# A residual block on eight cores: narrower weight chunks, saves of bf16 weights partly deferred and recorded later, constants on another queue, two x buffers in place of three

## Chip, cores, metric

The kernel runs on all 8 cores of one Trainium2 chip. Each core computes four of the 32 sequences, 16 tiles of 512 tokens, and exchanges no data with the others. The metric is the device time of the slowest core, in microseconds (us). Some runs fall in a second, slower state, in which one die's cores show a lower granted clock: one run of the kernel before took 4140 us with four cores at 0.834 to 0.839 and the other four at 0.983 to 0.987.

In the views, PE is TensorE (the matmuls), PEld its weight loads, DVE VectorE, ACT ScalarE, POOL GpSimd and SP SyncE. `wsrc` is the f32 source of the weights, `wbf` their bf16 copy in HBM, `ring` the slots on chip. The head is the time from the start to the merge stage of the second tile.

## The reference, cut to what matters

```python
xn  = rms_norm(h, norm_mix_pre)
proj = xn @ w_in                       # q, k, v, gMLP u and v, two gates: 1024 -> 3840
attn = banded_sink_attention(q, k, v)  # window 128, 8 query and 2 key heads
gm   = u * (W_s LN(v) + b)             # 128-token chunks
mix  = (sigmoid(g_a) * (attn @ w_a) + sigmoid(g_b) * (gm @ w_g)) @ w_out
h    = h + rms_norm(mix)
hn   = rms_norm(h)
ff   = (silu(hn @ w_gate) * (hn @ w_up)) @ w_down     # 1024 -> 2816 -> 1024
out  = h + rms_norm(ff)
# x is (32, 2048, 1024) float32, weights are float32, depth 1
```

## The kernel before

The weights are not kept on chip: every tile streams them through a ring of four slots, in 31 chunks. They arrive as f32 and are multiplied as bf16. In the first tile each chunk is loaded by a DMA that casts, issued from POOL, and then saved as bf16 in HBM by a DMA from SP. Later tiles reload the bf16 copy. The order of chunks in a tile is: merge M0 to M7, output projection O0 and O1, the next tile's Q, KV, U and VG, gate/up G0 to G10, and the six down chunks D0 to D5 twice (two halves of the tokens).

```python
NCH = 31
CHE = 4096
NSLOT = 4
NTMP = 10
N_CORES = 8
CAST_DMA = True
NXB = 3
# ...
    def record_load(self):
        n = self.n_loaded
        if n >= len(self.order):
            return
        self.n_loaded += 1
        c = self.order[n]
        s = n % NSLOT
        slot = self.ring[s]
        rkeys = [("ring", s, q4) for q4 in range(4)]
        if c not in self.cast_done:
            self.cast_done.add(c)
            if CAST_DMA:
                self.dma(AP(slot, CHE, 0, 128, 0, [(1, CHE)]), AP(self.wsrc_d, CHE, c * 128, 128, 0, [(1, CHE)]),
                         [], rkeys, ("WC", s), q="pool", max_last=8192)
            for q4 in (range(4) if not CAST_DMA else ()):
                si = self.stg_i
                self.stg_i = 1 - si
                stg = AP(self.stg[si], 1024, 0, 128, 0, [(1, 1024)])
                src = AP(self.wsrc_d, CHE, c * 128, 128, 1024 * q4, [(1, 1024)])
                self.dma(stg, src, [], [("stg", si)], ("ST", si))
                dst = AP(slot, CHE, 0, 128, 1024 * q4, [(1, 1024)])
                eng = ("dve", "act", "pool", "dve")[q4]
                if eng == "act":
                    fn = lambda e, o=dst, i=stg: e.activation(out=o, in_=i, func=AF.Copy)
                else:
                    fn = lambda e, o=dst, i=stg: e.tensor_copy(out=o, in_=i)
                self.op(eng, fn, [("stg", si)], [("ring", s, q4)])
            self.dma(AP(self.wbf_d, CHE, c * 128, 128, 0, [(1, CHE)]), AP(slot, CHE, 0, 128, 0, [(1, CHE)]),
                     rkeys, [("wbf", c)], ("WS", s))
        else:
            self.dma(AP(slot, CHE, 0, 128, 0, [(1, CHE)]), AP(self.wbf_d, CHE, c * 128, 128, 0, [(1, CHE)]),
                     [("wbf", c)], rkeys, ("W", s))
# (the branch for not CAST_DMA never runs)
    def chunk_done(self):
        while self.n_loaded < min(self.n_used + NSLOT, len(self.order)):
            self.record_load()
    def load_x(self, t):
        xb = self.xb[t % NXB]
        src = bass.AP(self.x_d, t * TT * D, [[D, 128], [128 * D, NB], [1, D]])
        dst = AP(xb, 4096, 0, 128, 0, [(D, NB), (1, D)])
        self.dma(dst, src, [], [("xb", t % NXB, b) for b in range(NB)], ("X", t % NXB))
    def store_y(self, t):
        xi = t % NXB
        xb = self.xb[xi]
        dst = bass.AP(self.y_d, t * TT * D, [[D, 128], [128 * D, NB], [1, D]])
        src = AP(xb, 4096, 0, 128, 0, [(D, NB), (1, D)])
        self.dma(dst, src, [("xb", xi, b) for b in range(NB)], [("y", t)], ("Y", xi))
# ...
    def record(self):
        n = self.n_tiles
        self.stream_init()
        self.load_x(0)
        self.load_consts(0)
        for _ in range(NSLOT - 1):
            self.record_load()
        self.rms_scale_all(0, 0)
        self.transposes(self.xnT, "xnT", self.g1, "g1")
        self.load_consts(1)
        self.stage_front(0)
        for t in range(1, min(n, NXB)):
            self.load_x(t)
        wo_groups = [[(C_O0, 8)], [(C_O0 + 1, 8)]]
        dn_groups = [[(C_D0, 8), (C_D0 + 1, 8), (C_D0 + 2, 6)], [(C_D0 + 3, 8), (C_D0 + 4, 8), (C_D0 + 5, 6)]]
        for _ in self.stage_attn(0):
            pass
        self.stage_spatial(0)
        for t in range(n):
            xi = t % NXB
            nxt = t + 1 < n
            self.stage_merge(t, inter=self.rms_scale((t + 1) % NXB, 0) if nxt else None)
            if t >= 1 and t - 1 + NXB < n:
                self.load_x(t - 1 + NXB)
            if nxt:
                self.transposes(self.xnT, "xnT", self.g1, "g1")
            self.tokmajor_out(xi, self.mergedT, "mg", wo_groups, self.g2bc, "g2bc", 16,
                              after_pair=lambda pair, xi=xi: self.rms_scale_all(xi, 1, (2 * pair, 2 * pair + 1)))
            hT = lambda: self.transposes(self.hnT, "hnT", self.g3, "g3")
            if nxt:
                self.stage_front(t + 1, mid=hT)
                self.stage_ffn_gu(t, mid=lambda t=t: self.stage_spatial(t + 1))
            else:
                hT()
                self.stage_ffn_gu(t)
            inter = self.stage_attn(t + 1) if nxt else None
            self.tokmajor_out(xi, self.hT, "h", dn_groups, self.g4bc, "g4bc", 16, inter=inter)
            self.store_y(t)
```

A wait is derived for each recorded operation from what it reads and writes, and each engine takes its operations strictly in recorded order. So a chunk's cast, on POOL, waits for the matmuls that read the slot's old chunk and for the save of that old chunk. A save, on SP, waits for its cast, and everything recorded later on SP waits behind it.

The softmax here doesn't subtract the row's maximum and nothing guards it: scores larger than these inputs give would overflow.

Of the kernel before, what the change touches and what calls it, by code (L numbers as in the profile page):

```python
# [23 lines left out]
CAST_DMA = True  # L24
NXB = 3
# [133 lines left out]

def build_wsrc(w_in, w_a, w_g, w_out, w_gate, w_up, w_down):  # L160
# [27 lines left out]
    return np.stack(chunks, axis=0)  # L188

def build_consts(norm_mix_pre, norm_mix_post, norm_ffn_pre, norm_ffn_post, attn_sinks,  # L190
# [6 lines left out]
    for g in range(2):  # L197
        for half in range(2):
            for hh2 in range(2):
# [20 lines left out]
    return {k: np.ascontiguousarray(v, dtype=np.float32) for k, v in c.items()}  # L220

CONST_SHAPES = {"ident": 128, "tbl": 2048, "g1": 8, "g3": 8, "g2bc": 1024, "g4bc": 1024,
                "lngpp": 4, "lnbpp": 4, "bsbc": 512, "sinkbc": 8, "wsT": 512, "cmask": 512}

class Builder:
# [7 lines left out]
    def alloc(self, es):  # L233
# [3 lines left out]
        self.wsrc_d = nc.dram_tensor("wsrc", [NCH * 128, CHE], F32, kind="ExternalInput")  # L237
# [23 lines left out]
        self.stg = [sb("stg%d" % i, 1024, F32) for i in range(2)] if not CAST_DMA else []  # L261
        self.stg_i = 0
# [6 lines left out]
        self.esink = sb("esink", 8, F32)  # L269
        self.wsT = sb("wsT", 512, BF16)  # L270
        self.ident = sb("ident", 128, BF16)
        self.ones = sb("ones", 128, BF16)
        self.g1 = sb("g1", 8, F32)
        self.g3 = sb("g3", 8, F32)
        self.lngpp = sb("lngpp", 4, F32)
        self.lnbpp = sb("lnbpp", 4, F32)
# [57 lines left out]

    def load_consts(self, part):
        ckey = ("C%d" % part,)
        def cdram(name, off=0, n=None):
            F = CONST_SHAPES[name]
            return AP(self.c_d[name], F, 0, 128, off, [(1, n or F)])

        def direct(name, t):
            n = CONST_SHAPES[name]
            self.dma(AP(t, n, 0, 128, 0, [(1, n)]), cdram(name), [], [("c", name)], ckey, bulk=True)

        def via_tmp(name, off, n):
            ti = self.ntmp()
            self.dma(self.T(ti, n), cdram(name, off, n), [], [("tmp", ti)], ckey, bulk=True)
            return ti

        if part == 0:  # L350
            for name, t in (("g1", self.g1), ("g3", self.g3), ("lngpp", self.lngpp), ("lnbpp", self.lnbpp)):
                direct(name, t)
        else:
            for name, t in (("g2bc", self.g2bc), ("g4bc", self.g4bc)):
                direct(name, t)
        if part == 0:
# [3 lines left out]
            ti = via_tmp("ident", 0, 128)  # L360
            self.op("dve", lambda e, o=AP(self.ident, 128, 0, 128, 0, [(1, 128)]), s=self.T(ti, 128):
                    e.tensor_copy(out=o, in_=s), [("tmp", ti)], [("c", "ident")])
        else:
            for q4 in range(4):
                ti = via_tmp("tbl", 512 * q4, 512)
                self.op("dve", lambda e, o=AP(self.tbl, 2048, 0, 128, 512 * q4, [(1, 512)]), s=self.T(ti):
                        e.tensor_copy(out=o, in_=s), [("tmp", ti)], [("c", "tbl")])
            ti = via_tmp("sinkbc", 0, 8)
            self.op("act", lambda e, o=AP(self.esink, 8, 0, 128, 0, [(1, 8)]), s=self.T(ti, 8):
                    e.activation(out=o, in_=s, func=AF.Exp), [("tmp", ti)], [("c", "esink")])  # L370
            self.op("dve", lambda e, o=AP(self.vtok, 650, 0, 128, 0, [(1, 650)]): e.memset(o, 1.0), [],
                    [("v", i) for i in range(5)])
            t3 = via_tmp("wsT", 0, 512)
            t4 = via_tmp("cmask", 0, 512)
            self.op("dve", lambda e, o=AP(self.wsT, 512, 0, 128, 0, [(1, 512)]), a=self.T(t3), b=self.T(t4):
                    e.tensor_tensor(out=o, in0=a, in1=b, op=ALU.mult), [("tmp", t3), ("tmp", t4)], [("c", "wsT")])
            t5 = via_tmp("bsbc", 0, 512)
# [3 lines left out]
            for g in range(4):  # L381
                self.op("dve", lambda e, o=AP(self.B2, 512, 0, 128, 128 * g, [(1, 128)]), i=self.P(bk, 128, 128 * g),
                        s=AP(self.lnbpp, 4, 0, 128, g, [(1, 1)]), b=self.T(t5, 128, off=128 * g):
                        e.scalar_tensor_tensor(out=o, in0=i, scalar=s, in1=b, op0=ALU.mult, op1=ALU.add),
                        [("ps", bk), ("c", "lnbpp"), ("tmp", t5)], [("c", "B2")])

    def stream_init(self):
# [10 lines left out]
        self.cast_done = set()  # L398
        self.n_loaded = 0
        self.n_used = 0  # L400

    def record_load(self):
        n = self.n_loaded
        if n >= len(self.order):
            return
        self.n_loaded += 1
        c = self.order[n]
        s = n % NSLOT
        slot = self.ring[s]
        rkeys = [("ring", s, q4) for q4 in range(4)]  # L410
        if c not in self.cast_done:
            self.cast_done.add(c)
            if CAST_DMA:
                self.dma(AP(slot, CHE, 0, 128, 0, [(1, CHE)]), AP(self.wsrc_d, CHE, c * 128, 128, 0, [(1, CHE)]),
                         [], rkeys, ("WC", s), q="pool", max_last=8192)
            for q4 in (range(4) if not CAST_DMA else ()):
                si = self.stg_i
                self.stg_i = 1 - si
                stg = AP(self.stg[si], 1024, 0, 128, 0, [(1, 1024)])
                src = AP(self.wsrc_d, CHE, c * 128, 128, 1024 * q4, [(1, 1024)])  # L420
                self.dma(stg, src, [], [("stg", si)], ("ST", si))
                dst = AP(slot, CHE, 0, 128, 1024 * q4, [(1, 1024)])
                eng = ("dve", "act", "pool", "dve")[q4]
                if eng == "act":
                    fn = lambda e, o=dst, i=stg: e.activation(out=o, in_=i, func=AF.Copy)
                else:
                    fn = lambda e, o=dst, i=stg: e.tensor_copy(out=o, in_=i)
                self.op(eng, fn, [("stg", si)], [("ring", s, q4)])
            self.dma(AP(self.wbf_d, CHE, c * 128, 128, 0, [(1, CHE)]), AP(slot, CHE, 0, 128, 0, [(1, CHE)]),
                     rkeys, [("wbf", c)], ("WS", s))  # L430
        else:
            self.dma(AP(slot, CHE, 0, 128, 0, [(1, CHE)]), AP(self.wbf_d, CHE, c * 128, 128, 0, [(1, CHE)]),
                     [("wbf", c)], rkeys, ("W", s))

    def next_chunk(self, expect):
# [3 lines left out]
        while self.n_loaded <= n:  # L439
            self.record_load()  # L440
        s = n % NSLOT
        return self.ring[s], [("ring", s, q4) for q4 in range(4)]

    def chunk_done(self):
        while self.n_loaded < min(self.n_used + NSLOT, len(self.order)):
            self.record_load()

    def load_x(self, t):
        xb = self.xb[t % NXB]
        src = bass.AP(self.x_d, t * TT * D, [[D, 128], [128 * D, NB], [1, D]])  # L450
        dst = AP(xb, 4096, 0, 128, 0, [(D, NB), (1, D)])
        self.dma(dst, src, [], [("xb", t % NXB, b) for b in range(NB)], ("X", t % NXB))

# [35 lines left out]
    def transposes(self, dst_t, dkey, gain, gname):  # L489
        for kc in range(8):  # L490
            bk = self.nbank()
            for b in range(NB):
# [7 lines left out]
            gsc = AP(gain, 8, 0, 128, kc, [(1, 1)])  # L500
            self.op("dve", lambda e, o=dst, i=src, s=gsc: e.tensor_scalar(out=o, in0=i, scalar1=s, scalar2=None,
                                                                          op0=ALU.mult),
                    [("ps", bk), ("c", gname)], [(dkey, kc)])
# [172 lines left out]
    def stage_spatial(self, t):  # L676
        for b in range(NB):
# [6 lines left out]
            for gq in range(4):  # L684
                self.op("dve", lambda e, o=self.T(tq, 128, off=128 * gq), i=self.P(bk, 128, 128 * gq),
                        s=AP(self.lngpp, 4, 0, 128, gq, [(1, 1)]), c=AP(self.B2, 512, 0, 128, 128 * gq, [(1, 128)]):
                        e.scalar_tensor_tensor(out=o, in0=i, scalar=s, in1=c, op0=ALU.mult, op1=ALU.add),
                        [("ps", bk), ("c", "lngpp"), ("c", "B2")], [("tmp", tq)])
# [6 lines left out]
    def stage_merge(self, t, inter=None, per_chunk=2):  # L695
        for c in range(8):
# [19 lines left out]
            if inter is not None and c >= 1:  # L716
                for _ in range(per_chunk):
                    next(inter, None)
# [102 lines left out]
    def store_y(self, t):  # L821
        xi = t % NXB
        xb = self.xb[xi]
        dst = bass.AP(self.y_d, t * TT * D, [[D, 128], [128 * D, NB], [1, D]])
        src = AP(xb, 4096, 0, 128, 0, [(D, NB), (1, D)])
        self.dma(dst, src, [("xb", xi, b) for b in range(NB)], [("y", t)], ("Y", xi))

    def record(self):
# [4 lines left out]
        for _ in range(NSLOT - 1):  # L833
            self.record_load()
        self.rms_scale_all(0, 0)
        self.transposes(self.xnT, "xnT", self.g1, "g1")
        self.load_consts(1)
        self.stage_front(0)
        for t in range(1, min(n, NXB)):
            self.load_x(t)  # L840
# [5 lines left out]
        for t in range(n):  # L846
            xi = t % NXB
            nxt = t + 1 < n
            self.stage_merge(t, inter=self.rms_scale((t + 1) % NXB, 0) if nxt else None)
            if t >= 1 and t - 1 + NXB < n:  # L850
                self.load_x(t - 1 + NXB)
            if nxt:
                self.transposes(self.xnT, "xnT", self.g1, "g1")
            self.tokmajor_out(xi, self.mergedT, "mg", wo_groups, self.g2bc, "g2bc", 16,
                              after_pair=lambda pair, xi=xi: self.rms_scale_all(xi, 1, (2 * pair, 2 * pair + 1)))
            hT = lambda: self.transposes(self.hnT, "hnT", self.g3, "g3")
# [7 lines left out]
            self.tokmajor_out(xi, self.hT, "h", dn_groups, self.g4bc, "g4bc", 16, inter=inter)  # L864
            self.store_y(t)
        self.op("sp", None, [("y", t) for t in range(n)], [])
# [70 lines left out]
```

## Time and profile before

| | |
|---|---|
| median of 6 runs, two of them slow | 3589.04 us (the four fast runs 3586.7 to 3590.2) |
| spans of the cores in the profiled run | 3573.9 to 3585.1 us, clock 0.984 to 0.988 |
| PE busy | 3388.8 us, 95% |
| queue of the casts (q0) | 6.3% of the 16 DMA engines' span |
| queue of SP (q1) | 59.3% |

The page of the kernel before divides the span into 40 slices of 90 us; a digit is a busy share in tenths.

```profile
span 3585.1 us, 53875 instructions; the slowest of 8 cores (3573.9 to 3585.1 us)
...
PE   3786899999999999999999999999999999999988
...
DMA  8989956758476574856657475665747557464645
```

PE is short of full in the first five slices and the last two; the DMA row is at 8 or 9 in the same first five. What PE waits for in the first 420 us is listed in the view of waits (engine and tile, what was waited for, us in total, times, longest):

```profile
PE ps L326 <- DMA ring<-wsrc: 56.9, 19, 5.3
PE ps L496 <- DVE xn L480: 34.0, 2, 33.7
PE ps L326 <- DVE wsT L376: 22.2, 1, 22.2
PE ps L326 <- DMA ring<-wbf: 6.1, 1, 6.1
```

The first row are casts that come late, one by one, the third is the constant `wsT`, which stands in PE's order before the first projection, and the last is the first reload of the second down pass.

### The profile page before, as it was taken

Reading aid. Unit: us, or ns where it says so; the run is one execution under the profiler, and the core shown is the slowest. Engines: PE = TensorE matmul, PEld = TensorE weight load, DVE = VectorE, ACT = ScalarE, POOL = GpSimd, SP = SyncE. Lnnn points to the kernel's source line nnn. Section 1 sums busy time; section 2 is a strip of 40 time slices with the busy share of each in tenths; the row PEclk is TensorE's granted clock in tenths of the full one; section 3 lists DMA queues with packets and bytes.
Section 4 is the critical chain, followed back from the end, with each engine's and each line's share of the span. In section 5 each row is a group of like instructions: output and inputs, shape, how many; then the busy total and the mean of one; then the engine's idle time right before and its main releaser. Section 6 shows DMA issues by size and latency. Waiting matters only on the chain.

```text
span 3585.1 us, 53875 instructions; the slowest of 8 cores (3573.9 to 3585.1 us)
## 1 busy us (share of the span) xinstructions
PE 3388.8 (95%) x18129; PEld 1587.2 (44%) x18129; DVE 1338.7 (37%) x2845; ACT 1046.9 (29%) x2130; POOL 408.7 (11%) x427
## 2 busy tenths in 40 slices
PE   3786899999999999999999999999999999999988
PEld 1342344444444444444444444444444444444433
DVE  1341352424435243443424335342443524244332
ACT  1321322323233232323323232332323223232321
POOL 1210110201001020100202011020201102010010
PEclk9899999999999999999999999999999999999999
DMA  8989956758476574856657475665747557464645
GB/s 186 217 190 212 268 180 198 231 168 251 160 232 195 188 244 155 251 167 222 207 183 246 148 250 174 211 221 172 254 153 246 177 200 230 169 225 162 229 144 193
DMA packets 113002, 726.82 MB, mean 203 GB/s; under 512 B 11360, under 2 KB 11488, under 8 KB 36960
## 3 DMA queue, kind: packets, MB, share of 16 engines
q1 hardware_dynamic: 104304, 690.87, 59.3%
q0 software_dynamic: 8432, 32.51, 6.3%
q8 instruction: 154, 2.52, 0.3%
q14 instruction: 112, 0.92, 0.1%
HBM read 689.78 MB, written 66.06 MB: 211 GB/s over the span
## 4 chain that ended last, share of the span: by engine, by line
PE 85%; DMA 8%; DVE 3%; issue 2%; ACT 1%; POOL 1%; SPq 0%; DVEq 0%; ACTq 0%; POOLq 0%
PE ps L326 83%; DMA ring<-wsrc 5%; DMA wbf<-ring 2%; PE ps L496 1%; DVE xb L793 1%; DVE tmp L773 1%; DMA tmp<-c_bsbc 1%; ACT atok L620 1%; PE ps L633 0%; ACT PT L661 0%; POOL stats L785 0%; DVE atok L624 0%; DMA ring<-wbf 0%; SPq L330 0%; DVE attnT L637 0%
## 5 line engine op out<-in xcount | busy, mean ns | idle before, releaser
L326 PE MATMUL ps<-hnT,ring 128*128 128x512 bf16 x5632 | 1224.6, 380 | 23.7 <-DMA ring<-wsrc 23.7
L326 PEld LDWEIGHTS ps<-hnT,ring 128*128 128x128 bf16 x5632 | 550.5, 98 | 688.5 <-issue 31.4
L326 PE MATMUL ps<-xnT,ring 128*128 128x512 bf16 x3328 | 750.8, 381 | 7.2 <-DMA ring<-wsrc 7.2
L326 PE MATMUL ps<-ring,hT 128*128 128x512 bf16 x2816 | 645.0, 383 | 30.4 <-DMA ring<-wsrc 20.6
L817 DVE TENSOR_TENSOR hT<-ps,tmp 128x512 bf16<-128x512 f32 x352 | 240.7, 691 | 798.9 <-PE ps L326 794.9
L326 PEld LDWEIGHTS ps<-xnT,ring 128*128 128x128 bf16 x3328 | 326.4, 98 | 401.7 <-issue 17.9
L813 ACT ACTIVATE tmp<-ps 128x512 f32<-128x512 f32 x352 | 210.2, 597 | 980.7 <-PE ps L326 974.0
L326 PEld LDWEIGHTS ps<-ring,hT 128*128 128x128 bf16 x2816 | 268.4, 99 | 340.6 <-issue 49.2
L785 POOL TENSOR_TENSOR stats<-stats,neghalf 128x2 f32<-128x2 f32 x64 | 44.9, 701 | 2080.9 <-DVE stats L782 2080.9
L326 PE MATMUL ps<-ring,mergedT 128*128 128x512 bf16 x1024 | 226.0, 381 | 7.8 <-DMA ring<-wsrc 5.3
L767 ACT ACTIVATE tmp<-ps 128x512 f32<-128x512 f32 x256 | 150.0, 595 | 262.8 <-PE ps L326 196.3
L710 DVE TENSOR_TENSOR tmp<-ps,tmp 128x512 f32<-128x512 f32 x128 | 88.4, 691 | 339.9 <-PE ps L326 333.2
L793 DVE SCALAR_TENSOR_TENSOR xb<-tmp,stats,xb 128x512 f32<-128x512 f32 x256 | 186.7, 750 | 75.1 <-POOL stats L785 61.1
L715 POOL TENSOR_TENSOR mergedT<-tmp 128x512 bf16<-128x512 f32 x128 | 166.5, 1300 | 413.8 <-DVE tmp L712 307.6
L661 ACT ACTIVATE PT<-ps 128x512 bf16<-128x512 f32 (+1 forms) x256 | 135.3, 581 | 203.9 <-PE ps L326 203.6
L464 ACT ACTIVATE xn<-xb 128x1024 bf16<-128x1024 f32 x128 | 134.3, 1051 | 154.5 <-DVE xb L793 154.4
L705 ACT ACTIVATE tmp<-ps 128x512 f32<-128x512 f32 x128 | 76.4, 597 | 278.9 <-PE ps L326 278.7
L326 PEld LDWEIGHTS ps<-ring,mergedT 128*128 128x128 bf16 x1024 | 100.0, 98 | 127.2 <-issue 11.6
L326 PE MATMUL ps<-ring,xnT 128*128 128x512 bf16 (+1 forms) x1024 | 144.3, 299 | 0.0
L326 PE MATMUL ps<-gmT,ring 128*128 128x512 bf16 x512 | 132.3, 381 | 4.1 <-DVE gmT L692 4.1
L326 PE MATMUL ps<-attnT,ring 128*128 128x512 bf16 x512 | 131.4, 379 | 0.0
L624 DVE TENSOR_SCALAR atok<-ps,stats 128x64 bf16<-128x64 f32 x256 | 72.7, 284 | 147.3 <-ACT atok L620 147.3
(68 smaller groups left out, 2048.3 us busy)
## 6 DMA issues: line engine op xcount, KB each, us to landing
ring<-wbf SPq DMA_DIRECT2D x561, 1024.0 KB, 6.1
xb<-x SPq DMA_DIRECT2D x16, 2048.0 KB, 12.8
y<-xb SPq DMA_DIRECT2D x16, 2048.0 KB, 10.6
ring<-wsrc POOLq DMA_DIRECT2D x31, 1024.0 KB, 24.5
wbf<-ring SPq DMA_DIRECT2D x31, 1024.0 KB, 12.4
tmp<-c_tbl SPq DMA_DIRECT2D x4, 256.0 KB, 21.8
g2bc<-c_g2bc SPq DMA_DIRECT2D x1, 512.0 KB, 12.8
g4bc<-c_g4bc SPq DMA_DIRECT2D x1, 512.0 KB, 19.1
```

What stands on the lines that cost most here:

```text
L326: self.op("pe", lambda e: e.matmul(out, lhsT, rhs, start=start, stop=stop), reads, writes)
L464: self.op("act", lambda e, o=junk, i=src, a=acc: e.activation(out=o, in_=i, func=AF.Square, accum_out=a), [("xb", xi, b)], [("xn", b), ("s ...
L624: e.tensor_scalar(out=o, in0=i, scalar1=s_, scalar2=None, op0=ALU.mult),
L661: e.activation(out=o, in_=s, func=AF.Exp, scale=0.125),
L705: self.op("act", lambda e, o=self.T(ta), s=self.P(bga): e.activation(out=o, in_=s, func=AF.Sigmoid), [("ps", bga)], [("tmp", ta)])
L710: e.tensor_tensor(out=o, in0=a, in1=c, op=ALU.mult), [("ps", bra), ("tmp", ta)], [("tmp", t1)])
L715: e.tensor_tensor(out=o, in0=a, in1=c_, op=ALU.add), [("tmp", t1), ("tmp", t2)], [("mg", c)])
L767: e.activation(out=o, in_=i, func=AF.Square, accum_out=a),
L785: self.op("pool", lambda e, o=ms, h=nh: e.tensor_tensor(out=o, in0=o, in1=h, op=ALU.pow), [mkey, ("c", "neghalf")], [mkey])
L793: e.scalar_tensor_tensor(out=o, in0=i, scalar=s, in1=x_, op0=ALU.mult, op1=ALU.add),
L813: self.op("act", lambda e, o=self.T(tg), s=self.P(bg): e.activation(out=o, in_=s, func=AF.Silu), [("ps", bg)], [("tmp", tg)])
L817: e.tensor_tensor(out=o, in0=a, in1=c, op=ALU.mult),
```

## The change

Its intent is to shorten the start. It (1) stores the source without padding and moves only the used columns of a chunk, (2) casts odd gate/up chunks again in the second tile and saves them only then, (3) records a save three chunks later, (4) issues constants from ACT, packs the small ones, consumes them in the middle of the first projections, and issues chunks 1 to 3 behind the first normalisation, (5) keeps two x buffers, so the next x is loaded in the merge stage behind the old tile's store, and splits loads and stores of a tile by 128-token block. The core of the diff, with cuts:

```diff
-CAST_DMA = True
-NXB = 3
+NXB = 2
# ...
+def SAVE_AT(c):
+    return 0 if c >= C_D0 or c < C_G0 or c % 2 == 0 else 1
+
+CW = ([4096, 3072, 4096, 4096] + [3072] * 8 + [4096] * 2 + [4096] * 11 + [4096, 4096, 3072] * 2)
+OFF = [128 * sum(CW[:c]) for c in range(NCH)]
+NW = 128 * sum(CW)
# ...
-    return np.stack(chunks, axis=0)
+    return np.concatenate([np.ascontiguousarray(ch[:, :CW[c]]).reshape(-1) for c, ch in enumerate(chunks)]).reshape(-1, PW)
# ... (constants: q="act"; tables loaded in part 1, consumed in part 2)
+    def rkeys(self, n):
+        return [("ring", n % NSLOT, q4) for q4 in range(4)]
+
+    def issue(self, q="sp"):
+        n = self.n_issued
+        self.n_issued += 1
+        self.flush(n - 3)
         c = self.order[n]
         s = n % NSLOT
# ... (record_load removed)
+        if self.kind[n] == "bf":
+            self.dma(AP(self.ring[s], CHE, 0, 128, 0, [(1, CW[c])]), AP(self.wbf_d, CHE, c * 128, 128, 0, [(1, CW[c])]),
+                     [("wbf", c)], self.rkeys(n), ("W", s), q=q)
+            return
+        self.dma(AP(self.ring[s], CHE, 0, 128, 0, [(1, CW[c])]),
+                 bass.AP(self.wsrc_d, OFF[c], [[CW[c], 128], [1, CW[c]]]), [], self.rkeys(n), ("WC", s), q="pool", max_last=8192)
+        if self.kind[n] == "cast_save":
+            self.unsaved.append(n)
+
+    def flush(self, upto):
+        while self.unsaved and self.unsaved[0] <= upto:
+            n = self.unsaved.pop(0)
+            c, s = self.order[n], n % NSLOT
+            self.dma(AP(self.wbf_d, CHE, c * 128, 128, 0, [(1, CW[c])]), AP(self.ring[s], CHE, 0, 128, 0, [(1, CW[c])]),
+                     self.rkeys(n), [("wbf", c)], ("WS", s))
+
+    def advance(self):
+        k, total = self.n_used, len(self.order)
+        while True:
+            m = self.n_issued
+            if m >= total or m >= k + NSLOT:
+                break
+            self.issue()
 
     def load_x(self, t):
-        xb = self.xb[t % NXB]
-        src = bass.AP(self.x_d, t * TT * D, [[D, 128], [128 * D, NB], [1, D]])
-        dst = AP(xb, 4096, 0, 128, 0, [(D, NB), (1, D)])
-        self.dma(dst, src, [], [("xb", t % NXB, b) for b in range(NB)], ("X", t % NXB))
+        xi = t % NXB
+        for b in range(NB):
+            src = bass.AP(self.x_d, (t * TT + 128 * b) * D, [[D, 128], [1, D]])
+            dst = AP(self.xb[xi], 4096, 0, 128, D * b, [(1, D)])
+            self.dma(dst, src, [], [("xb", xi, b)], ("X", xi, b))
+
+    def store_y(self, t, blocks):
+        xi = t % NXB
+        for b in blocks:
+            dst = bass.AP(self.y_d, (t * TT + 128 * b) * D, [[D, 128], [1, D]])
+            src = AP(self.xb[xi], 4096, 0, 128, D * b, [(1, D)])
+            self.dma(dst, src, [("xb", xi, b)], [("y", t, b)], ("Y", xi, b))
 
# ...
-    def stage_merge(self, t, inter=None, per_chunk=2):
+    def stage_merge(self, t, inter=None, load=None, start=4, per_chunk=3):
-            if inter is not None and c >= 1:
+            if load is not None and c == 1:
+                load()
+            if inter is not None and c >= start:
                 for _ in range(per_chunk):
# ...
     def record(self):
         n = self.n_tiles
         self.stream_init()
         self.load_x(0)
         self.load_consts(0)
-        for _ in range(NSLOT - 1):
-            self.record_load()
+        self.issue(q="act")
+        self.load_consts(1)
         self.rms_scale_all(0, 0)
-        self.transposes(self.xnT, "xnT", self.g1, "g1")
-        self.load_consts(1)
-        self.stage_front(0)
-        for t in range(1, min(n, NXB)):
-            self.load_x(t)
+        self.advance()
+        self.transposes(self.xnT, "xnT", "g1")
+        self.stage_front(0, mid=lambda: (self.load_consts(2), self.load_x(1)))
         wo_groups = [[(C_O0, 8)], [(C_O0 + 1, 8)]]
         dn_groups = [[(C_D0, 8), (C_D0 + 1, 8), (C_D0 + 2, 6)], [(C_D0 + 3, 8), (C_D0 + 4, 8), (C_D0 + 5, 6)]]
         for _ in self.stage_attn(0):
@@ -846,14 +871,13 @@
         for t in range(n):
             xi = t % NXB
             nxt = t + 1 < n
-            self.stage_merge(t, inter=self.rms_scale((t + 1) % NXB, 0) if nxt else None)
-            if t >= 1 and t - 1 + NXB < n:
-                self.load_x(t - 1 + NXB)
+            self.stage_merge(t, inter=self.rms_scale((t + 1) % NXB, 0) if nxt else None,
+                             load=(lambda t=t: self.load_x(t + 1)) if nxt and t > 0 else None)
             if nxt:
-                self.transposes(self.xnT, "xnT", self.g1, "g1")
+                self.transposes(self.xnT, "xnT", "g1")
             self.tokmajor_out(xi, self.mergedT, "mg", wo_groups, self.g2bc, "g2bc", 16,
                               after_pair=lambda pair, xi=xi: self.rms_scale_all(xi, 1, (2 * pair, 2 * pair + 1)))
-            hT = lambda: self.transposes(self.hnT, "hnT", self.g3, "g3")
+            hT = lambda: self.transposes(self.hnT, "hnT", "g3")
             if nxt:
                 self.stage_front(t + 1, mid=hT)
                 self.stage_ffn_gu(t, mid=lambda t=t: self.stage_spatial(t + 1))
@@ -861,9 +885,9 @@
                 hT()
                 self.stage_ffn_gu(t)
             inter = self.stage_attn(t + 1) if nxt else None
-            self.tokmajor_out(xi, self.hT, "h", dn_groups, self.g4bc, "g4bc", 16, inter=inter)
-            self.store_y(t)
-        self.op("sp", None, [("y", t) for t in range(n)], [])
+            self.tokmajor_out(xi, self.hT, "h", dn_groups, self.g4bc, "g4bc", 16, inter=inter,
+                              after_pair=lambda pair, t=t: self.store_y(t, (2 * pair, 2 * pair + 1)))
+        self.op("sp", None, [("y", t, b) for t in range(n) for b in range(NB)], [])
         self.S.finalize()
 
```

## The prediction

> **What bounds the kernel now.** I read the page first, then busy times by stretches, then the chain of waits through the first 400 us, then the DMA queues, the waits of one steady stretch, and the order in which SP meets its DMA issues. Columns of the first fence: stretch, its length, busy us of each engine with instruction count, granted TensorE clock, DMA share, GB/s.
>
> ```profile
> 0.00:50.00 50.00, 4.04 (x32) 3.33 (x32) 6.25 (x14) 5.55 (x9) 7.42 (x11) 1.00 0.97 209
> 50.00:100.00 50.00, 33.07 (x184) 15.25 (x185) 14.36 (x40) 13.40 (x26) 5.08 (x8) 0.96 0.76 167
> ...
> 200.00:250.00 50.00, 47.21 (x270) 23.31 (x269) 27.98 (x62) 16.63 (x32) 12.46 (x17) 0.97 0.84 163
> 250.00:300.00 50.00, 36.76 (x169) 15.95 (x167) 9.37 (x16) 5.97 (x10) 3.57 (x5) 1.00 1.02 212
> 300.00:350.00 50.00, 34.31 (x145) 14.09 (x144) 4.84 (x7) 6.55 (x10) 3.57 (x5) 0.93 1.02 212
> ...
> 700.00:3400.00 2700.00, 2671.48 (x14435) 1255.30 (x14434) 1055.97 (x2254) 828.74 (x1685) 295.76 (x303) 1.00 0.62 202
> ```
>
> From 700 to 3400 us PE is busy 2671 of 2700 us at full clock with the DMA engines 62% busy: that part is bound by PE, and nothing in the diff removes a matmul. In the first 400 us the DMA share is near 1 while PE idles: that part is bound by DMA. By count, 14435 matmuls take 2700 us, 0.187 us each, so all 18129 would take 3391; about 195 us of the 3585 are start and end, and only these can shrink.
>
> The chain (start, duration, what) shows what the start waits for:
>
> ```profile
> 61.68 28.04 PE ps L326 x145
> ...
> 124.56 8.89 PE ps L326 x28
> ...
> 133.98 14.80 DMA ring<-wsrc
> 148.83 12.91 DMA wbf<-ring
> ...
> 162.34 24.51 DMA ring<-wsrc
> ...
> 213.74 11.08 DMA ring<-wsrc
> ...
> 358.94 24.32 DMA ring<-wsrc
> ...
> 383.83 9.48 DMA ring<-wbf
> ```
>
> The first projection matmul waits until 61.7 (VectorE is held by constants whose loads stand behind weight saves on SP). The merge stage starts at 124.6. Then the chain alternates cast load (f32 weight to bf16 ring) and save (ring to the bf16 copy), because a ring slot may be refilled only when its save has landed. The last cast lands at 383.3; the first reload, issued only then, lands at 393.3.
>
> The DMA queues from 250 to 300 us give prices:
>
> ```profile
> q0 software_dynamic: 1382, 5.32, 75.2%
> q1 hardware_dynamic: 720, 5.24, 26.5%
> ```
>
> q0 has the casts: 75.2% of 50 us for 5.32 MB of 1.05 MB chunks, so 7.4 us of all 16 engines each. q1 has the saves: 26.5% for five chunks, 2.65 us each. From 700 to 3400 the hardware queue moved 543.78 MB in a 61.8% share: 3.07 us per MB, 3.2 us per reloaded chunk. Check: from 213.7 to 383.3 there are 17 casts and 16 saves, 126 + 42 = 168 us; measured 169.6. So work in DMA time predicts this stage.
>
> **What the Trainium skill says.** "DMA: Bandwidth & Descriptors", section "SWDGE vs HWDGE vs iDMA": a cast during DMA can be issued from GpSimd only. So the casts remain on POOL, as in both kernels. Same page, "Issuing engines are not separate DMA queues": issue from a second engine saves sequencer time, not transfer time; hence constants on ACT's queue are no more bandwidth, only freedom from SP's order. The trace agrees in that the two queues above sum to about 100%. Same page, "Queues, rings and completion order": each DMA engine round-robins between rows that have work. In 0 to 50 us the trace has 50.0% software to 47.1% hardware. Same page, "Anatomy of one DMA": about 2.0 us plus bytes over 436 GB/s. For the last 2 MB store that is 6.8 us; the trace has 3577.4 to 3585.1.
>
> **The change part by part.**
>
> *1. Narrow chunks.* Padding goes: KV, eight merge chunks and two down chunks are 3072 wide. 11 of 31 chunks lose a quarter: 28.25 chunk equivalents, 2.75 x 7.4 = 20 us less casting, 7 us less saving. The same in steady tiles is hidden.
>
> *2. Five saves deferred.* Odd gate/up chunks are cast in tile 0 without a save and cast again, with save, in tile 1: 13 us less in the head; in tile 1 five casts and saves in place of five reloads, 5 x (7.4 + 2.65 - 3.2) = 34 us more DMA work.
>
> *3. Constants on ACT, first chunk ahead, the rest behind the first normalisation; two x buffers.* Also one x load less in the head (6.4 us), and saves recorded three chunks later, so that a reload no longer stands behind the newest save on SP.
>
> I now walk the head; a sum of gains would ignore stretches in which the ring is full and DMA idles.
>
> Start to merge. x (6.4 us of work) shares the engines with two other rows and lands about 21, where it landed at 16.3 beside one; squares, scaling and transposes add 10 us, so projections begin near 31, no longer held by constants. But they are held by their weights. Up to the landing of chunk VG: casts 3.75 x 7.4 = 27.8, x 6.4, constants 2.97 MB x 3.07 = 9.1, three saves 7.3, start 2.5, an estimated gap of 1.5 before chunks 1 to 3 are issued: 54.6. VG's matmuls 7.1, attention and spatial gating as now (89.3 to 124.6) 35.2: merge starts at 97. Before 124.6. In that time the ring fills with M0 to M3, so DMA idles some 10 us; this limits the gain.
>
> Merge to landing of O1. M0 takes 5.2, so M4's cast is issued at 102. Then casts 4 x 5.55 + 2 x 7.4 = 37.0, saves 10.6, and two reloads (Q, KV) that now come earlier, 5.6: 155. Before: 129.8 to 186.9, 57 us; 53 now.
>
> O1 to the first gate/up cast: PE, ACT, DVE and POOL in series, 213.7 - 186.9 = 26.9, unchanged (POOL's order is the same there): 182.
>
> Gate/up and down: casts (11 + 5.5) x 7.4 = 122, six even gate/up saves 16, four down saves 10, two early reloads 6.4, start 1.7: 156, so the last cast lands at 338. Before 169.6. D5's matmuls run at once and the next chunk is already there: the second pass begins at 341.5, before at 393.6. Gain 52 us.
>
> End: the final store is split, and only blocks 2 and 3 are left for the end. By the formula above one 0.5 MB store needs 3.2 us plus issue 0.4: about 3.5 us gained.
>
> Tile 1: gate/up there is 11 x 6.9 = 76 us of PE. DMA: six reloads 19 plus five cast-and-saves 50 = 69 us. It fits, but barely. A cast is issued three chunks (20.7 us) before use and needs at most some 15 us with its neighbours. Loss: 2 us.
>
> Steady tiles with two x buffers and split stores:
>
> ```profile
> 1058.16 0.39 SPq L330 DMA_DIRECT2D y<-xb  x1
> 1058.70 35.18 SPq L330 DMA_DIRECT2D ring<-wbf  x8
> 1093.97 1.55 SPq L330 DMA_DIRECT2D xb<-x  x1
> ```
>
> Before, x comes 36 us after the store and two tiles ahead. After, it is issued in the same tile at merge chunk 1, about 1062 on this scale, and each block waits for its own store. The last store is issued at 1058.6 and lands about 1065; x lands by 1075 to 1079. Its first reader is now at merge chunk 4 (1077), its last Square at 1082, and the transposes at 1093: xn is done about 1092. Tight, but no wait. The store of blocks 0 and 1 makes SP wait for xb at 1036.8, so the fifth down chunk of the second half is issued 6 us later than now, behind 1 MB of store, and lands about 1046; PE wants it at 1045.8. An estimated 0.2 us per tile, 3.5 in all.
>
> Sum: 3589 - 52 - 3.5 + 2 + 3.5 = 3539; I say **3538 us**, 1.4% faster.
>
> **Rivals.**
>
> *The work simply goes.* 27 + 13 + 6 us of DMA work, 10 us of DMA idleness (61 to 71, ring full and no tile of x due) and 7 us after the last cast would give 63 us, with the tail 66: 3523. For: the DMA share is 1.02 where the chain alternates. Against: the ring of four fills during attention and at O, and DMA idles there whatever was saved earlier.
>
> *SP's order becomes the new wait.* With two buffers x stands on SP in front of weight loads and waits for stores. If store and load took the 10.6 and 12.8 us that whole-tile transfers take, last block and weight M6 would be late by some 3 us per tile: 15 x 3 = 45 us, gain eaten: 3580. For: SP takes its issues in order, and PE has almost no slack. Against: each block is a quarter of that size, and M6 isn't needed until 1083.
>
> *Tile 1 saturates.* If the second casts take the 24.5 us of the head, five of them late by 4 us cost 20: 3558. Against: 24.5 us was measured with two queues saturated; the shortest cast landed in 10.1 us.
>
> **Range and chances.** The head's terms reproduce the old stage within 2 us, but the idle stretches are chosen, so +-10; steady tiles 0 to +1 us each, 0 to 15; tile 1 0 to 10. That makes 3518 to 3560. 2% is 3519 in round numbers; the first rival would nearly reach it: 0.10 faster, 0.89 same, 0.01 slower.
>
> **What would show it.** Right: the first projection matmul near 31 us, merge from about 97, the last first-pass cast landed near 338, second down pass directly behind; saves gone from the odd gate/up chunks, five casts in tile 1 with no PE wait on them; tiles at 211 to 212 us apart as now; last store about 4 us. Wrong: PE waiting in steady tiles for ring reloads at the fifth down chunk, or for VectorE's xn before the transposes; merge later than 105; tile 1's gate/up longer than 80 us.

## The result, and the profile after

Median 3537.31 us in 8 timed runs (3532.7 to 3542.5) against 3587.7, the median of the ten fast runs of the kernel before in the same rounds (3588.7 with its six slow ones). Ratios in this document are the mean time of one kernel's fast runs over that of the other's in the same rounds, so not quite the ratio of the medians. Here it is 0.986, 95% interval 0.9849 to 0.987: by the 2% rule "same", but clear of noise. The prediction was 3538, inside 3518 to 3560.

From the page of the changed kernel:

```profile
span 3535.9 us, 54133 instructions; the slowest of 8 cores (3517.7 to 3535.9 us)
...
PE   4896999999999999999999999999999999999988
...
DMA  9799787456464644747455464644737465464635
```

Busy times by stretch (columns as in the prediction; the engines in the order PE, PEld, DVE, ACT, POOL):

```profile
0.00:50.00 50.00, 21.02 (x133) 12.08 (x134) 11.64 (x24) 8.76 (x14) 8.86 (x13) 1.00 0.95 216
50.00:100.00 50.00, 31.66 (x201) 14.56 (x200) 23.87 (x77) 21.77 (x45) 3.66 (x6) 0.83 0.87 212
...
150.00:200.00 50.00, 43.29 (x238) 21.14 (x239) 22.32 (x46) 17.21 (x35) 10.48 (x14) 0.90 0.66 154
200.00:250.00 50.00, 44.48 (x209) 19.75 (x208) 18.07 (x37) 8.23 (x14) 5.62 (x8) 0.97 1.03 181
...
700.00:3400.00 2700.00, 2664.15 (x14362) 1249.92 (x14360) 1047.86 (x2228) 826.70 (x1695) 304.78 (x308) 1.00 0.56 188
```

PE has 133 matmuls behind it at 50 us where it had 32. From 200 to 300 us the DMA share is 1.03, as it was 1.02 from 250 to 350 us before, but 150 to 200 shows 0.66: around the end of the output projection and the next tile's projections DMA idles a third of the time. The steady stretch is PE-bound as it was, with 56% DMA in place of 62%.

The chain of waits of the changed kernel (start, duration, what):

```profile
99.42 28.62 PE ps L335 x124
...
128.58 27.89 DMA ring<-wsrc
...
156.71 12.87 PE ps L335 x48
...
183.54 10.31 DMA ring<-wsrc
...
314.11 24.83 DMA ring<-wsrc
...
339.07 5.47 PE ps L335 x26
...
369.76 41.60 PE ps L335 x192
```

This is the head of the prediction, station by station, each read on the slowest core of its own profile:

| station | before | predicted | after |
|---|---|---|---|
| first projection | 62.1 | near 31 | 30.8 |
| cast of VG landed, PE goes on | – | 54.6 | 55.0 |
| chain enters the merge | 124.6 | 97 | 99.4 |
| O1 landed | 187.1 | 155 | 156.7 |
| first gate/up cast issued | 213.7 | 182 | 183.5 |
| last cast of the first pass landed | 383.3 | 338 | 339.0 |
| second down pass begins | 393.6 | 341.5 | 345.0 |
| second tile's merge begins | 416.8 | – | 369.8 |

Averaged over all eight cores, the second tile's merge begins at 412.9 before and at 362.8 after: the head is 50 us shorter. But for 1.8 us in the last tile, nothing comes back later. On core 1 the last stores of tile 1 and of tile 0 are 212.0 us apart before and 211.7 after, the following thirteen tiles take 2754.1 before and 2753.3 after. So the mean granted clock, 0.984 to 0.988 before and 0.989 to 0.990 in the profiled run after, is not where the gain comes from. In the steady stretch of the changed kernel no wait of PE for a DMA is listed. Two lines from the order of operations at the very end (start, duration, engine, line, operation, idle time before it):

```profile
3520.58 6.20 PE L335 MATMUL ps<-ring,hT 128*128 128x512 bf16 x28 [1.83 <-DMA ring<-wbf]
...
3531.38 1.85 SPq L339 DMA_DIRECT2D y<-xb  x2
```

The first is the fifth down chunk of the second half, late by 1.8 us, in the last tile only: there the attention of a next tile, which gives the reload time elsewhere, is missing. The second is the final store. VectorE ends at 3532.8 and the span at 3535.9, 3.1 us later; before it was 3577.3 and 3585.1, 7.8 us.

### The profile page after: what moved, and what is told of

Same layout as the page of the kernel before. It is cut to its first block, busy times and chain, and to the rows that moved or that the text cites. A ratio compares the mean times of both kernels' runs of the same rounds, so it can differ in the third digit from the quotient of the medians.

```text
span 3535.9 us, 54133 instructions; the slowest of 8 cores (3517.7 to 3535.9 us)
## 1 busy us (share of the span) xinstructions
PE 3384.5 (96%) x18129; PEld 1586.2 (45%) x18129; DVE 1337.9 (38%) x2845; ACT 1046.1 (30%) x2131; POOL 413.1 (12%) x432
## 4 chain that ended last, share of the span: by engine, by line
PE 85%; DMA 7%; DVE 4%; issue 2%; ACT 1%; POOL 1%; DVEq 0%; SPq 0%; ACTq 0%; POOLq 0%
PE ps L335 83%; DMA ring<-wsrc 4%; PE ps L528 2%; DMA wbf<-ring 1%; DVE xb L827 1%; DVE tmp L807 1%; DMA ring<-wbf 1%; ACT atok L652 1%; DMA xb<-x 1%; PE ps L665 0%; ACT PT L693 0%; DVE atok L656 0%; POOL stats L819 0%; ACT tmp L801 0%; DVE attnT L669 0%
## 5 line engine op out<-in xcount | busy, mean ns | idle before, releaser
L652 ACT ACTIVATE atok<-ps,stats 128x64 bf16<-128x64 f32 x256 | 80.9, 316 | 164.8 <-DVE stats L646 92.9
```

What stands on the lines that cost most here:

```text
L652: e.activation(out=o, in_=i, func=AF.Copy, scale=s_),
```

## The experiments

Twelve kernels ran. Most alter the changed kernel in one place. Times are medians of fast runs, and "us slower" or "faster" is the difference of two ratios to the kernel before times 3587 us. The intervals of two ratios together make such a difference uncertain by 6 to 9 us.

### The changed kernel again (control)

> The changed kernel unaltered, as a control on the chip of the next three runs. Expected: the ratio of its first timing, 0.985 to 0.987 of the kernel before.

Ratio 0.9863 (0.9844 to 0.9881), two fast runs, 3536.2 us. As in the first timing (the experiments ran on four chips, each beside the kernel before).

### The constants alone

The kernel before, with part 4 of the change only (without packing the small ones):

```diff
-            self.dma(..., cdram(name), [], [("c", name)], ckey, bulk=True)
+            self.dma(..., cdram(name), [], [("c", name)], ckey, bulk=True, q="act")
 # tables: loaded in load_consts(1), consumed in load_consts(2)
         self.load_consts(0)
-        for _ in range(NSLOT - 1):
-            self.record_load()
+        self.load_consts(1)
+        self.record_load()
         self.rms_scale_all(0, 0)
+        for _ in range(NSLOT - 2):
+            self.record_load()
         self.transposes(self.xnT, "xnT", self.g1, "g1")
-        self.load_consts(1)
-        self.stage_front(0)
+        self.stage_front(0, mid=lambda: self.load_consts(2))
```

> The kernel before with one part of the change alone: constants issued on ACT's queue and consumed in the middle of the first projections, first chunk ahead of the normalisation. Projections near 31 us instead of 61.7. If earlier PE work only helps by removing idle DMA time (10 us around 61 to 71, some 6 us in attention): 15 us faster than before, near 3573. Rival, the 28 us won up to the merge stay to the end: near 3561.

Measured 3568.8 us, ratio 0.9956 (0.9941 to 0.9971): 15.8 us faster. Projections begin at 32 us. Its chain of waits:

```profile
102.52 7.68 PE ps L326 x28
...
110.73 21.75 DMA ring<-wsrc
...
341.14 22.95 DMA ring<-wsrc
...
364.66 8.62 DMA ring<-wbf
```

The merge is entered at 102.5 and not 124.6, 22 us earlier, and the first reload of the second pass lands at 373.3 and not 393.3, 20 us earlier in this profile and about 16 in the timing. So the rival's 28 us are out, but because only 22 were won up to the merge: of these nearly all stay. The cause given, that only idle DMA time is won, isn't shown by the size that it hit (15 predicted). On the mean of the cores the DMA engines idle 28.3 us of the head before and 19.9 here, 8 us less; the rest of the 21 us won there is that the same 87 MB kept them busy 13 us less. Why, stays open.

### The padding restored

```diff
-CW = ([4096, 3072, 4096, 4096] + [3072] * 8 + [4096] * 2 + [4096] * 11 + [4096, 4096, 3072] * 2)
+CW = [4096] * 31
```

> The changed kernel with every weight chunk 4096 wide again (padding restored, everything else kept). My walk through the head: one more 1.85 us cast and 0.65 us save before the merge, the four early merge chunks land in the stretch in which DMA idles (about 10 us) and cost nothing, merge to O1 plus 10.8 us, gate/up and down plus 5 us: about 18 us slower than the changed kernel, so near 3555. Rival, all DMA work counts: 27 us slower, near 3564. Steady tiles unchanged in both.

Measured 3542.2 us (three fast runs), ratio 0.9878 (0.986 to 0.9896): 6.5 us slower, at the edge of noise (the second merge begins 7.3 us later on the mean of the cores). Both theories miss, mine by a factor of nearly three. The DMA queue of the casts from 0 to 345 us, first of this kernel, then of the changed one (packets, MB written, share of the 16 engines):

```profile
q0 software_dynamic: 8432, 32.51, 62.3%
```

```profile
q0 software_dynamic: 8432, 29.62, 59.8%
```

In both, all 31 casts of the first pass lie in this window. 62.3% of 345 us is 214.9 us for 31 full chunks, 6.93 each; 59.8% is 206.3 us for 28.25 equivalents, 7.30 each. On the mean of the eight cores it is 6.90 and 7.16, so 31 x 6.90 - 28.25 x 7.16 = 12 us of cast time were taken away by narrowing, where 20 were counted. The difference is not in the narrow chunks alone: between 220 and 280 us, where both kernels cast full chunks, the price was 6.81 with padding and 7.07 without. The traces also give the split. Up to the second merge, on the mean of the cores, padding keeps the DMA engines busy 17 us longer (12 on the casts' queue, 5 on the others) where 27 were counted, and they idle 9.6 us less, where 10 were counted. So the absorption into idle time was right, and the work was mis-sized.

### Narrow chunks, but read from padded rows

One difference between the two is where the bytes lie: packed, a chunk has rows of 12 KB and starts at any multiple of 0.5 MB. This kernel reads 12 KB out of rows of 16 KB.

```diff
-OFF = [128 * sum(CW[:c]) for c in range(NCH)]
-NW = 128 * sum(CW)
+OFF = [128 * CHE * c for c in range(NCH)]
+NW = 128 * CHE * NCH
-                 bass.AP(self.wsrc_d, OFF[c], [[CW[c], 128], [1, CW[c]]]), ...
+                 bass.AP(self.wsrc_d, OFF[c], [[CHE, 128], [1, CW[c]]]), ...
```

> The changed kernel with narrow chunks read from the padded source: row pitch 16 KB and 2 MB per chunk in HBM as before the change, 12 KB of each row read. Restoring the padding as a whole had cost 6.5 us and not the 18 of my walk, and its casts took about 6.8 us per full chunk against 7.0 to 7.5. If it is the packed layout in HBM that makes casts dearer, this kernel has the narrow chunks and the cheap casts: 28 x 0.4 = 11 us less DMA time in the head, some 8 us faster than the control. Rival, layout is not it: within 3 us of the control, and the cheaper casts come from something else.

Ratio 0.9853 (0.9834 to 0.9871), two fast runs, against 0.9863 of the control in the same rounds: 3.6 us faster, inside the intervals. The price over 0 to 345 us was 7.05 us per full-chunk equivalent on the mean of eight cores, against 7.21 for the control and 6.90 with all chunks full. From 220 to 280 us it was 6.86, against 7.08 for the control. So the layout may be a part of it, but the time doesn't prove it, and the kernel before, with the padded layout too, paid 7.37 in its 220 to 280 us. A queue's share also counts time in which packets of another queue were under way (the two summed to 101.7% from 250 to 300 us before), so a part of a price may be what ran beside the casts; that was not tested. Why casts are dearer in one kernel than in another stays open.

### All saves in the first tile

```diff
 def SAVE_AT(c):
-    return 0 if c >= C_D0 or c < C_G0 or c % 2 == 0 else 1
+    return 0
```

> The changed kernel with all 31 saves in the first tile (no second casts in tile 1). Five saves of 2.65 us return to the gate/up stretch, which is saturated: 12 to 13 us slower than the changed kernel, near 3550; tile 1 keeps its length. Rival, second casts in tile 1 cost PE time: then it is slower by less than 12, because tile 1 gets shorter.

Measured 3547.4 us, ratio 0.9891 (0.9878 to 0.9905): 11 us slower. The second merge begins at 376.0 on the mean of the cores, 13.2 later than in the changed kernel. Deferral is worth what 5 x 2.65 said, and the second casts cost tile 1 nothing measurable: it takes 211.7 us with and without them (core 1).

### All gate/up chunks deferred

```diff
-    return 0 if c >= C_D0 or c < C_G0 or c % 2 == 0 else 1
+    return 1 if C_G0 <= c < C_D0 else 0
```

> The changed kernel with all eleven gate/up chunks cast unsaved in tile 0 and cast with save in tile 1 (the change does so with five). Six more saves leave the head: 16 us. In tile 1 gate/up then needs 11 x (7.4 + 2.65) = 110 us of DMA against 76 us of PE: about 30 us of waits for casts there. Net 14 us slower than the changed kernel, near 3551. Rival, second casts are hidden whatever their number: 16 us faster, near 3521.

Fast runs 3539.4, 3543.8, 3546.1 and 3585.2; the last has one die at clock 0.976 against 0.989 of the other. With it the ratio is 0.9916 (0.9872 to 0.9961). The median is 3544.9, which over the 3583.5 median of before is 0.989, some 11 us slower than the changed kernel. The second merge begins at 341.4 on the mean, 21 us earlier. On core 0 tile 1 then takes 243.1 us in place of 211.7; on the mean of the cores 238.8. Its gate/up stage, first of this kernel and then of the changed one:

```profile
429.00:537.00 108.00, 84.34 (x368) 36.09 (x367) 25.78 (x50) 15.02 (x24) 7.19 (x11) 0.94 1.01 226
```

```profile
454.00:532.00 78.00, 78.00 (x375) 35.82 (x373) 26.07 (x52) 15.02 (x24) 4.57 (x7) 1.00 0.80 213
```

With eleven casts the stage takes 108 us at a DMA share of 1.01 (110 us of DMA were predicted); with five it takes 78 at 0.80 and PE never stops. The predicted 30 us in tile 1 are there (31.4 on core 0, 27 on the mean). So the five deferred chunks are within the free DMA time of one tile, and eleven are not.

### The save directly behind its cast

```diff
         if self.kind[n] == "cast_save":
             self.unsaved.append(n)
+            self.flush(n)
```

> The changed kernel with each save recorded directly behind its cast, as before the change, so that the first reload of the second down pass again stands on SP behind the last save. If that wait is what the later recording takes away: PE waits about 6 us for that reload, 7 us slower, near 3544. Rival, from my own accounting: the early reloads only move 12 us of DMA work from idle stretches into saturated ones, and the kernel gets 5 us faster, near 3532.

Measured 3529.1 us, ratio 0.984 (0.9826 to 0.9853): 7 us faster than the changed kernel, just clear of noise. The wait that the later recording removes does come back, shown at the start of the second down pass:

```profile
319.03 2.75 PE L335 MATMUL ps<-ring,hT 128*128 128x512 bf16 x12 [1.59 <-DMA ring<-wsrc]
...
327.45 6.14 PE L335 MATMUL ps<-ring,hT 128*128 128x512 bf16 x16 [4.34 <-DMA ring<-wbf]
```

PE waits 4.3 us for the first reload, but the last cast landed at 319 on this core, and the second merge begins at 353.8 on the mean, 9 us earlier. The rival was right. SP issues reloads of the changed kernel while casts are still to come (its D5 cast lands at 339):

```profile
138.09 0.32 SPq L339 DMA_DIRECT2D ring<-wbf  x1
...
319.08 0.32 SPq L339 DMA_DIRECT2D ring<-wbf  x1
...
329.38 0.32 SPq L339 DMA_DIRECT2D ring<-wbf  x1
```

In this variant they come in two groups, at 150.9 after the last cast for the output projection and from 319.5 after the last cast of all. On the mean of the cores the DMA engines do the same work in the head (332.0 us busy against 330.7) and idle 21.8 us in place of 32.1. Part 3 of the change, taken out by itself, gains 7 us.

### Three x buffers

```diff
-NXB = 2
+NXB = 3
-        self.stage_front(0, mid=lambda: (self.load_consts(2), self.load_x(1)))
+        self.stage_front(0, mid=lambda: (self.load_consts(2), self.load_x(1), self.load_x(2)))
-                             load=(lambda t=t: self.load_x(t + 1)) if nxt and t > 0 else None)
+                             load=(lambda t=t: self.load_x(t + 2)) if t + 2 < n and t > 0 else None)
```

> The changed kernel with three x buffers again, the x of tile t+2 loaded in the merge of tile t, so that x is never late; stores stay split. If two buffers cost in steady tiles as I estimated (0.2 us each), within 3 us of the changed kernel, and one more x load in the head (6.4 us of DMA) falls into a stretch with idle DMA. Rival, SP held by x costs 3 us a tile: up to 45 us faster.

Measured 3532.5 us, ratio 0.9857 (0.9843 to 0.987): 1 us faster, within noise. Two buffers cost the steady tiles nothing measurable.

### Six ring slots

The buffer that was freed has the size of two ring slots.

```diff
-NSLOT = 4
+NSLOT = 6
```

> The changed kernel with a ring of six slots instead of four (the second x buffer freed the room). If the ring's four slots are what lets DMA idle during attention (about 10 us) and at the output projection (13 us and more, as the first gate/up cast can then be issued when O ends and not behind the POOL chain), the head gets about 20 us shorter: near 3517, and the 1.8 us wait for a reload in the last tile goes. Rival, only the sum of DMA work counts: within 3 us of the changed kernel.

Measured 3513.7 us (three fast runs), ratio 0.9796 (0.978 to 0.9812): 23 us faster than the changed kernel. It is 2.04% faster than the kernel before, but the interval holds 2%, so by the 2% rule the verdict is "unclear". Busy times of this kernel in the two stretches in which DMA had idled:

```profile
50.00:100.00 50.00, 31.45 (x209) 14.71 (x207) 23.86 (x77) 22.26 (x46) 3.66 (x6) 0.84 1.03 206
150.00:200.00 50.00, 49.45 (x259) 23.52 (x260) 25.07 (x53) 18.87 (x37) 13.24 (x18) 0.91 0.83 171
```

The DMA share rises from 0.87 to 1.03 and from 0.66 to 0.83, that is by 8 us in each. The second merge begins at 342.6 on the mean, 20 us earlier, and of the head's 32 us of idle DMA time 4.6 are left. The wait for a reload in the last tile is gone from the list of waits. So the four slots, not the amount of DMA work alone, set the length of the head.

### Six slots with the other two

Six slots and the save directly behind its cast; six slots and padded rows; all three. The edits are those above.

> Six ring slots and saves directly behind their casts, the two variants that were faster by 23 and 7 us. If both gains come from moving DMA work into idle stretches they overlap: 23 to 27 us faster than the control, near 3511. Rival, independent: 30 us, near 3507. Second rival: with six slots a save directly behind its cast holds reloads on SP longer, and it is slower than six slots alone.

Ratio 0.9782 (0.9768 to 0.9795), 3506.5 us: 29 us faster than the control. That is nearer to independent gains than to overlapping ones, but the difference is uncertain by some 8 us and holds both; only the second rival, slower than six slots alone, is unlikely.

> Six ring slots with the padded source rows. If the layout theory holds, 8 us faster than six slots alone, near 3506; if not, the six-slot time again, near 3514.

Ratio 0.9788 (0.9772 to 0.9803), 3509.7 us: 27 us faster than the control, 3 faster than six slots alone were in other rounds. Not resolved.

> Six slots, saves directly behind their casts, padded source rows: all three variants that were faster. If the padded rows' 3 us are real and independent, 3 us faster than six slots with early saves, a ratio near 0.977; rival, they were noise: 0.978 to 0.9785.

Ratio 0.9776 (0.9759 to 0.9794), 3507.2 us. The lowest ratio of all, but its interval covers that of six slots with early saves. The padded rows stay unproven; six slots are not.

## Why the prediction was right

**The bound.** The first 383 us are bound by DMA work that can be summed, the rest by PE. Shown: the gains and losses of the variants lie in the head, except where eleven second casts overload tile 1.

**The walk through the head.** Predicted 52 us gained at the second pass, measured 48.5 on the slowest cores (393.6 to 345.0) and 50 at the second merge on the mean. Every station is within 3.5 us. (The walk's "merge starts" is where the chain enters it: PE had run M0's first 20 matmuls from 115.6 and then waited for VectorE's `gmT`, 4.1 us before and 3.1 after.) That DMA idles in spite of the work that waits is shown by the shares of 0.87 (6 us idle of 50) and 0.66 (17 us) and by six slots. The idle time was put at 10 us for attention and was not put in a number for the output projection, but is contained in its unchanged 26.9 us. The rival "the work simply goes" (3523) fell by this: it let idle time go with the work, and the head idles 32.1 us after the change against 28.3 before.

**The parts of it.** The table is read from the DMA queues of all eight cores, on the mean, from the start to the second merge. Busy is the sum of the queues' shares of the 16 engines times the time. In full stretches that sum reaches 1.03, so idle time is understated by a few us.

| kernel | second merge, us | busy, us | idle, us | MB |
|---|---|---|---|---|
| before | 412.9 | 384.6 | 28.3 | 87.3 |
| constants alone | 391.8 | 371.9 | 19.9 | 87.4 |
| changed | 362.8 | 330.7 | 32.1 | 73.8 |
| changed, again | 365.2 | 333.0 | 32.2 | 73.6 |
| padding restored | 370.1 | 347.6 | 22.5 | 80.5 |
| all saves in the first tile | 376.0 | 342.8 | 33.2 | 79.2 |
| save at once | 353.8 | 332.0 | 21.8 | 73.9 |
| six slots | 342.6 | 338.0 | 4.6 | 74.9 |

The change takes 54 us of DMA work out of the head and adds 4 us of idle time: the 50 us are less work. The casts' queue does 20.5 us less (222.7 to 202.2), as the 20 predicted. The others do 33.5 less, where 7 + 13 + 6.4 = 26.4 were predicted; constants alone show 8 us less there with the same bytes, which the prediction did not count.

Deferral: 12 to 13 predicted, 11 measured. Constants: no number of its own, but as a run 15 predicted, 15.8 measured, only in part for the reason given (8 us of idle time, where 16 were counted). Padding: as a part taken out of the changed kernel its worth was wrong, 18 us against 6.5, because with padding restored casts are cheaper than in either main kernel, 6.90 us against 7.17 and 7.16. It did no harm to the walk, which priced the changed kernel's casts at 7.4, near the 7.30 that its slowest core paid. The later saves: rightly put as two early reloads of 5.6 and 6.4 us against the removed wait; the variant shows the trade as a loss of 7 us.

**What isn't explained.** The four parts as measured, 15.8 + 6.5 + 11 - 7, sum to 26 of the 51 us. They need not add up: one was put into the kernel before, three were taken out of the changed one, each shifts idle time as well as work, and the split of the final store is in none of them. Why the same bytes keep the engines busy for less time in one kernel than in another is not shown by any run.

**Tile 1 and steady tiles.** Predicted 2 and 3.5 us lost; measured none, and 1.8 us in the last tile, at the very chunk that was named as tight. The rival that SP's order becomes the new wait (3580) fell by the three-buffer run, the one that tile 1 saturates (3558) by its 211.7 us.

**The end.** Predicted 3.5 us gained, measured 4.7 (7.8 to 3.1). The 3.2 us in it was an estimate with the formula of "Anatomy of one DMA", which the page gives for DMAs issued from GpSimd; this store is issued from SP.

**Slips without effect.** 2% of 3589 puts the bar at 3517, not 3519. The 50.0% to 47.1% of 0 to 50 us do not test how the engines share between queues: from 250 to 300 us the same two had 75.2% and 26.5%.

The hits and misses cancel in part: the head was 2 to 3.5 us worse than said, tile 1 and the steady tiles 5 us better, the last tile 2 us worse. The agreement within 1 us of the total is luck, that within 4 us at each station is not.

## What to carry to other kernels

Where a stage is bound by transfers, walk it station by station and note where the ring is full: work removed before such a point is worth only a part (7 of 17 us for the padding), unless the ring can run further ahead, and memory freed elsewhere may be worth most as further slots (23 us here). Move deferred transfers only into as much idle queue time as the next stage has, and count it: five chunks were free, eleven cost 27 us on the mean of the cores. Letting one kind of transfer overtake another is a trade, and has to be measured by itself.

## What the Trainium skill lacked or had wrong

- "DMA: Bandwidth & Descriptors" names who may issue a cast but gives no speed for it. A cast of 2 MB f32 to 1 MB bf16 kept the 16 engines busy 6.8 to 7.4 us (means of the cores, by kernel and stretch), against 3.2 us for a 1 MB reload. That fits a price by the bytes read, about 290 GB/s of source (2.1 MB in 7.2 us), a little below the 326 GB/s of the steady stretch.
- The same page has nothing on how much the price of such a cast differs by core. In the kernel before it was 7.00 to 7.30 us over 0 to 345 us. The two cores with the cheapest casts (7.00 and 7.02) began the second merge at 406.4 and 405.1, six others at 410.6 to 416.8. In the changed kernel two cores at 7.30 began it at 369.8 and 367.8, three at 7.01 to 7.03 at 355.0 to 359.5. So the head's spread over the cores goes with it; which causes which was not tested, and the cheap cores are not the same in both kernels (2 and 7, then 0, 3 and 7).
- Same page, "Anatomy of one DMA": its formula is fitted on DMAs issued from GpSimd. Used for a store from SP it gives an estimate of 3.2 us for 0.5 MB, and 3.2 us is the median in the trace of the changed kernel. For 2 MB the estimate is 6.8, and the last store of the kernel before ended 7.7 us after its issue began.
